# SiLU by one ScalarE function, and decay matrices of all heads formed beside the first stage and kept in DRAM

## The chip, the cores and the metric

The kernel runs on one core of a Trainium2 chip. The metric is the device time of one execution in microseconds, as the median of several runs. The engines are PE (TensorE, matrix products), DVE (VectorE), ACT (ScalarE), POOL (GpSimd) and SP (SyncE, which here only issues DMAs). Each works through its own instructions in the order of the program and waits on semaphores for the others. ACT and POOL issue DMAs too.

## The reference

One decoder block with two token mixers over 512 tokens of 2048 channels, in fp32: an mLSTM with 8 heads and a gated DeltaNet with 16 heads of 128 channels, which share one input projection and one output projection. Cut to what the change touches:

```python
def _causal_conv_silu(x, w):               # q, k and v of the DeltaNet
    y = sum(w[j] * xp[:, j:j + s] for j in range(kw))
    return jax.nn.silu(y)

# DeltaNet, per head: gam = cumsum of the log decay g over a chunk of 64 tokens
rel = gam[..., :, None] - gam[..., None, :]
decay_mat = jnp.where(incl, jnp.exp(jnp.where(incl, rel, 0.0)), 0.0)
a_mat = jnp.where(strict, bc[..., :, None] * kk * decay_mat, 0.0)
qk = jnp.einsum('cbhtd,cbhsd->cbhts', qc, kc) * decay_mat

# mLSTM, per head, with b the cumsum of log f and i the input gate
dmat = jnp.where(causal, bcum[..., :, None] - bcum[..., None, :] + ic[..., None, :], -jnp.inf)
intra_w = jnp.exp(dmat - m_t[..., None]) * scores
```

The decay matrices depend on the gates alone, which come from a narrow projection at the start; q, k and v are not needed for them. The kernel forms them in tiles of 128 tokens, so that a head has four matrices of 128x128, 256 KB together.

## The kernel before, in words

**Stages.** The front (0 to 135 us) loads x, forms the normalised `u`, the gates (`gates`) and a first part of q and k. The seven stage (135 to about 1105 us) computes the wide projections (output gates, SiLU paths, one part of q and k, v, merge gates). The mixers (to about 1870 us) run the heads in pairs beside the rest of the projections. The output stage (to about 2105 us) multiplies by the output weights.

**Products.** An fp32 weight tile is split in two parts of a shorter format: `wh` is ACT's cast (L143), `wl` DVE's difference (L146). Each product is then three matmuls, L614 with `wh` and the high part of `u`, L615 with `wl`, L616 with the low part of `u`.

**The seven stage** works through 13 blocks (`SEVEN`) of two column groups of 512; blocks 9 to 12 are the merge gates (kind "g"). A block replaces eight products of quarters by seven and has 16 quads of weights: eight A quads with four products each (m6, m1, m5, m7), then eight B quads with three. A product is six matmuls, two halves `t` of 128 rows by three, and takes 1.36 us; an A quad takes 5.44, a block 76.2. For an A quad DVE forms the sums `t` (128x1024, L555) and `ts` (128x512, L556) from the raw weights `wr`; ACT and DVE split `ts`, a part of `wr` and `t`. For a B quad DVE forms `ts` (L574), and the wide part is `wr` itself. The raw weights come through SP's queue into a ring of four buffers (tag "wr").

**Where a block turns.** The sums of products stand in banks `ps`: m6 in two, m1, m5 and m7 in two each, one for each half `t`. After the eighth A quad (the turn from A to B) ACT copies m6 to `X` (L599), and DVE adds m1, m5 and m7 to copies in `X` (L671), so that the B products can write the banks. At the end of a block the results are evacuated: those of m1 and m5 by ACT straight from the bank into a tile `to` (L682, `out_`), those of m7 by DVE into `X` and then ACT in place (L687, `late`). Each is stored with a DMA on ACT's queue, for the merge gates to `tg_d`. A tile `to` is a buffer of the same ring "wr" as the raw weights. The banks pass from block to block in turn: the m7 products of the next block write the banks that held m5.

**Order.** PE's instructions are written out by hand. The other engines' instructions are ordered by the scheduler from priorities (`urgent`, `behind`). `start(gen, ...)` runs a generator beside PE's products: `tick()` is called once for each product, and a `yield n` puts the rest off by n ticks. `beside[b]`, filled from `ahead`, is the generator that starts during block b; before, only the scaling of `u` and its loading back run in this way.

**Mixers.** `silu_end` takes a convolved tile to SiLU: with weights that were halved before, ACT's Tanh into `th` (L930), then DVE's (th + 1) · x (L931). `dn_front_k` broadcasts a head's row of `gam` to all partitions by a DMA on POOL's queue (`gb`), POOL masks it (L974, `affine_select`), ACT takes four exponentials of 128x128 (L985); the second head of a pair takes four of 64x64 more (L988), for a block of the matrix with its sign turned, and both one over the whole row (L990). `ml_head` does the same from `nrb` into `wm` (L1267, L1272).

## Time and profile before

| | us |
|---|---|
| median of 3 runs (lowest, highest) | 2138.02 (2137.24, 2138.37) |
| the profiled execution's own time | 2138.79 |
| its span, first to last instruction | 2137.0 |
| PE busy | 2117.4 (99%) |
| DVE busy | 1736.5 (81%) |
| ACT busy | 1084.7 (51%) |
| POOL busy | 473.1 (22%) |

The times in the trace start with the span, and an execution takes about 1.8 us more than it. Busy is the time in which an engine had an instruction under way; matmuls are pipelined, so a busy PE is not one at its peak. The granted clock of PE was 0.998 of full speed over the span. DMA moved 463 MB, 217 GB/s.

### The profile page before, as it was taken

The numbers are of one execution on the slowest core, as the hardware profiler recorded it, in microseconds if no ns is written. First come the engines' busy times: TensorE is split into PE (matmuls) and PEld (weight loads), VectorE is DVE, ScalarE is ACT, GpSimd is POOL, SyncE is SP. The second block draws the span as 40 slices with busy tenths as digits, with TensorE's granted clock in tenths as the row PEclk, the third lists the DMA queues.
The fourth block names the chain that finished last, engine by engine and source line by source line (L and its number), as shares of the span: only waits on it lengthen the run. The fifth ranks groups of instructions, "written<-read, shape, count | busy, mean of one in ns | idle before, by whom it ended". The sixth has DMA issues, their size and how long they took to land.

```text
span 2137.0 us, 32335 instructions
## 1 busy us (share of the span) xinstructions
PE 2117.4 (99%) x10555; PEld 1753.1 (82%) x10555; DVE 1736.5 (81%) x3024; ACT 1084.7 (51%) x2107; POOL 473.1 (22%) x681
## 2 busy tenths in 40 slices
PE   9999999999999999999999999999999999999998
PEld 7778888888888888888888888888888888887786
DVE  5988898898888888777857887887878888569887
ACT  4445555455554554444445556556465464345345
POOL 1210000000004000000003345345344363243211
PEclk9999999999999999999999999999999999999999
DMA  5456766677778877776987777678786678678895
GB/s 178 142 182 205 225 217 224 228 232 239 230 246 254 256 223 230 238 225 197 308 293 184 188 181 189 164 181 190 190 217 169 167 193 220 187 237 276 247 295 228
DMA packets 459203, 463.39 MB, mean 217 GB/s; under 512 B 198357, under 2 KB 306618, under 8 KB 458906
## 3 DMA queue, kind: packets, MB, share of 16 engines
q1 hardware_dynamic: 385466, 347.71, 56.4%
q0 software_dynamic: 25472, 75.26, 11.4%
q10 hardware_dynamic: 48096, 38.36, 5.4%
q8 instruction: 83, 1.36, 0.3%
q14 instruction: 86, 0.70, 0.1%
HBM read 359.41 MB, written 105.97 MB: 218 GB/s over the span
## 4 chain that ended last, share of the span: by engine, by line
PE 85%; DMA 3%; DVE 3%; issue 1%; ACT 1%; SPq 0%; POOL 0%; ACTq 0%; POOLq 0%; DVEq 0%
PE ps L615 17%; PE ps L614 17%; PE ps L616 17%; PE pj L265 14%; PE pj L263 7%; PE py L1494 2%; PE py L1496 2%; PE py L1495 2%; DMA ls<-ld 1%; DVE wl L146 1%; PE pqk L1077 1%; PE pnum L1300 1%; PE po L1189 1%; PE pw L1174 1%; PE pr L1166 1%
## 5 line engine op out<-in xcount | busy, mean ns | idle before, releaser
L143 ACT CAST wh<-wr 128x512 fp32r<-128x512 f32 (+1 forms) x522 | 374.2, 718 | 414.0 <-PE pj L265 199.3
L146 DVE TENSOR_TENSOR wl<-wr,wh 128x512 fp32r<-128x512 f32 (+1 forms) x522 | 442.3, 849 | 147.0 <-ACT wh L143 137.3
L263 PE MATMUL pj<-uh,wh 128*128 128x512 f32 x896 | 375.9, 420 | 1.3 <-ACT qk L379 1.3
L265 PE MATMUL pj<-uh,wl 128*128 128x512 f32 x896 | 351.4, 392 | 0.6 <-DVE wl L146 0.6
L265 PE MATMUL pj<-ul,wh 128*128 128x512 f32 x896 | 349.9, 390 | 0.3 <-DVE ul L330 0.3
L615 PE MATMUL ps<-wl,uh 128*128 128x512 f32 x752 | 292.7, 389 | 1.4 <-DVE wl L146 1.4
L614 PE MATMUL ps<-wh,uh 128*128 128x512 f32 x752 | 292.7, 389 | 0.8 <-DVE X L671 0.8
L616 PE MATMUL ps<-wh,ul 128*128 128x512 f32 x752 | 292.6, 389 | 0.0
L143 ACT CAST wh<-t 128x1024 fp32r<-128x1024 f32 x120 | 126.5, 1054 | 285.8 <-PE ps L616 153.3
L569 POOL DMA_DIRECT2D t_d<-ts x104 | 56.7, 545 | 863.8 <-DVE ts L556 831.7
L615 PE MATMUL ps<-wl,suh 128*128 128x512 f32 x624 | 242.9, 389 | 0.8 <-DVE wl L146 0.8
L614 PE MATMUL ps<-wh,suh 128*128 128x512 f32 x624 | 242.9, 389 | 0.2 <-ACT wh L143 0.2
L616 PE MATMUL ps<-wh,sul 128*128 128x512 f32 x624 | 242.7, 389 | 0.0
L143 ACT CAST wh<-ts 128x512 fp32r<-128x512 f32 x240 | 148.2, 618 | 173.9 <-DVE ts L574 149.0
L146 DVE TENSOR_TENSOR wl<-t,wh 128x1024 fp32r<-128x1024 f32 x120 | 146.9, 1224 | 77.2 <-ACT wh L143 77.1
L265 PEld LDWEIGHTS pj<-uh,wl 128*128 128x128 f32 x896 | 168.2, 188 | 37.0 <-DVE wl L146 1.0
L263 PEld LDWEIGHTS pj<-uh,wh 128*128 128x128 f32 x896 | 168.9, 188 | 31.1 <-ACT qk L379 1.8
L265 PEld LDWEIGHTS pj<-ul,wh 128*128 128x128 f32 x896 | 169.0, 189 | 30.6 <-DVE ul L330 1.1
L146 DVE TENSOR_TENSOR wl<-ts,wh 128x512 fp32r<-128x512 f32 x240 | 164.5, 686 | 21.0 <-ACT wh L143 19.5
L615 PEld LDWEIGHTS ps<-wl,uh 128*128 128x128 f32 x752 | 141.2, 188 | 31.2 <-DVE wl L146 2.0
L614 PEld LDWEIGHTS ps<-wh,uh 128*128 128x128 f32 x752 | 141.1, 188 | 30.6 <-DVE X L671 1.2
L616 PEld LDWEIGHTS ps<-wh,ul 128*128 128x128 f32 x752 | 141.1, 188 | 29.3
(363 smaller groups left out, 3898.0 us busy)
## 6 DMA issues: line engine op xcount, KB each, us to landing
wr<-in_w_in_dram SPq DMA_DIRECT2D x744, 256.0 KB, 3.9
wr<-in_w_out_dram SPq DMA_DIRECT2D x138, 256.0 KB, 4.7
t_d<-ts POOLq DMA_DIRECT2D x104, 256.0 KB, 3.8
wr<-t_d SPq DMA_DIRECT2D x104, 256.0 KB, 4.1
us_d<-uhi ACTq DMA_DIRECT2D x16, 256.0 KB, 3.5
us_d<-ulo ACTq DMA_DIRECT2D x16, 256.0 KB, 4.8
tg_d<-X ACTq DMA_DIRECT2D x16, 256.0 KB, 4.5
tg_d<-to ACTq DMA_DIRECT2D x16, 256.0 KB, 4.6
```

The costliest lines, as they stand in the source:

```text
L143: newest["A"] = A.copy(hi, src).ins
L146: newest["V"] = V.tensor_tensor(out=lo, in0=src, in1=hi.bitcast(F32), op=ALU.subtract).ins
L263: T.matmul(ps[j], hi[:, k, wsl], uh[:, kt, :], start=(kt == 0), stop=False)
L265: T.matmul(ps[j], w[:, k, wsl], x_[:, kt, :], start=False, stop=(kt == KT - 1 and w is lo))
L569: queue.dma_start(t2_d[b % 2, i], ts[:, 0, :])
L614: T.matmul(ps[t], ah, hi, start=(g == "A" and i == 0), stop=False, skip_group_check=True)
L615: T.matmul(ps[t], ah, lo, start=False, stop=False, skip_group_check=True)
L616: T.matmul(ps[t], al, hi, start=False, stop=(i == KH - 1), skip_group_check=True)
L1077: T.matmul(pk[:, c, :], kq[j][:, 0, tsl], kq[j][:, 1, tsl], start=True, stop=True)
L1494: T.matmul(ps[c], uh[:, kt, tsl], hi, start=(kt == ks[0]), stop=False)
L1495: T.matmul(ps[c], uh[:, kt, tsl], lo, start=False, stop=False)
L1496: T.matmul(ps[c], ul[:, kt, tsl], hi, start=False, stop=(kt == ks[-1]))
```

## The change

`silu_end` uses ACT's Silu in place, without DVE's multiplication and without the halved weights. The program has two table loads on ACT in place of one, the second ahead of the first Silu. A new generator `decay(n)` forms the decay matrices of head n in a buffer `spare(False)` of the ring "wr": the row's broadcast on POOL's queue, the mask on POOL three ticks later, the exponentials on ACT two ticks later, and a store to `dm_d` on ACT's queue. It runs for the 24 heads one after the other, six ticks each, from the eighth quad of block 9 on (`ahead[KH + 1]`). For the odd DeltaNet heads (`mirror`) it takes twelve exponentials, four of 64x128 and eight of 64x64, for the others four of 128x128. In the mixers `load_decay` loads them on SP's queue. `gates` takes the exponential of all `gam` rows once and stores it as rows 33 to 48.

```diff
     def silu_end(dst, then=None):
-        th = wkb.tile([P, S], F32, tag="th", name="th", bufs=2)
         with behind("A"):
-            A.activation(th, dst, AF.Tanh)
-        V.scalar_tensor_tensor(out=dst, in0=th, scalar=1.0, in1=dst, op0=ALU.add, op1=ALU.mult)
+            A.activation(dst, dst, AF.Silu)
...
         nc.scalar.dma_start(rows_d[16:32, :], gam)
+        A.activation(gr, gam, AF.Exp)
+        nc.scalar.dma_start(rows_d[33:49, :], gr)
...
+    def decay(n):
+
+        mirror = n < DNH and n % 2
+        bias, row = (ngam[:, :, n], 16 + n) if n < DNH else (acol[:, :, n - DNH], n - DNH)
+        flat = spare(False)
+        t = flat.rearrange("p (c t) -> p c t", t=P)
+        G.dma_start(flat, rows_d[row, :].partition_broadcast(P))
+        if mirror:
+            pgam = sbp.tile([P, NC], F32, tag="pgam", name="pgam", bufs=1)
+            G.tensor_scalar(out=pgam, in0=bias, scalar1=-1.0, scalar2=None, op0=ALU.mult)
+        yield 3
+        for a, b in (((0, 0), (64, 64)) if mirror else ((0, 0),)):
+            v = t[a:(a + 64 if mirror else P), :, b:P]
+            G.affine_select(out=v, in_=v, pattern=[[0, NC], [1, P - b]], channel_multiplier=-1, base=0,
+                            compare_op=ALU.is_ge, fill=-1e30)
+        yield 2
+        with behind("A"):
+            for c in range(NC):
+                if mirror:
+                    A.activation(t[0:64, c, :], t[0:64, c, :], AF.Exp, bias=bias[0:64, c:c + 1])
+                    A.activation(t[64:P, c, 64:P], t[64:P, c, 64:P], AF.Exp, bias=bias[64:P, c:c + 1])
+                    A.activation(t[64:P, c, 0:64], t[64:P, c, 0:64], AF.Exp, scale=-1.0, bias=pgam[64:P, c:c + 1])
+                else:
+                    A.activation(t[:, c, :], t[:, c, :], AF.Exp, bias=bias[:, c:c + 1])
+            nc.scalar.dma_start(dm_d[n], flat)
+        yield 1
+
     ahead = [None] + [scaled_u(k) for k in range(0, KT, 2)] + [None] * (len(SEVEN) - KH - 1)
+
+    def decays():
+        for n in range(DNH + MLH):
+            yield from decay(n)
+
+    ahead[KH + 1] = decays()
...
+    def load_decay(t, n):
+        with behind("S"):
+            nc.sync.dma_start(t.rearrange("p c t -> p (c t)"), dm_d[n])
...
     def dn_front_k(hs, kq, u):
-        rbs = [row_bcast(16 + h, "gb") for h in hs]
-        yield 4
+        rbs = [row_bcast(33 + h, "gb") for h in hs]
         for j in range(2):
             dm = wk.tile([P, NC, P], F32, tag="dm", name="dm")
-            G.affine_select(out=dm, in_=rbs[j], pattern=[[0, NC], [1, P]], channel_multiplier=-1, base=0,
-                            compare_op=ALU.is_ge, fill=-1e30)
+            load_decay(dm, hs[j])
             u["dm"].append(dm)
...
-            with behind("A"):
-                for c in range(NC):
-                    A.activation(dm[:, c, :], dm[:, c, :], AF.Exp, bias=ngam[:, c, h:h + 1])
-                if j:
-                    for c in range(NC):
-                        A.activation(dm[64:128, c, 0:64], rb[64:128, c, 0:64], AF.Exp, scale=-1.0,
-                                     bias=pgam[64:128, c:c + 1])
-                A.activation(rb, rb, AF.Exp)
...
-        rb = row_bcast(h, "nrb")
...
-        G.affine_select(out=w, in_=rb, pattern=[[0, NC], [1, P]], channel_multiplier=-1, base=0,
-                        compare_op=ALU.is_ge, fill=-1e30)
+        load_decay(w, DNH + h)
         yield 2
-        with behind("A"):
-            for c in range(NC):
-                A.activation(w[:, c, :], w[:, c, :], AF.Exp, bias=acol[:, c, h:h + 1])
```

Three places in ACT's order follow. In such rows a DMA waits for the last transfer that used its own semaphore, so that "DMAHW7" at a store says which semaphore it takes, and "DMAHW7" at a later row that it waits for this store. Lines of the changed kernel are numbered higher by three (L685 for L682, L690 for L687, L602 for L599). `to<-to` are the exponentials of `decay`, in a tile of the ring.

ACT at the end of block 9, before. The casts are those of the next block's first weights.

```order
L143 CAST wh<-t_7934 128x1024 [waits PE_49,Activation_49]
L687 ACTIVATE X<-X,bia 128x512 x2
L682 ACTIVATE to<-ps,bia 128x512 [waits PE_49] x2
...
L683 DMA tg_d<-to 128x512 [waits DMAHW5_49,Activation_49]
L682 ACTIVATE to<-ps,bia 128x512 [waits DVE_49]
...
L143 CAST wh<-t_8013 128x1024 [waits DVE_49,PE_49]
...
L682 ACTIVATE to<-ps,bia 128x512 [waits DVE_49]
L143 CAST wh<-ts 128x512 [waits DVE_49,PE_49]
L143 CAST wh<-wr_7923 128x512 [waits DMAHW2_49,PE_49]
...
L687 ACTIVATE X<-X,bia 128x512 [waits DVE_49] x2
```

The same place in the changed kernel; twelve exponentials (4 of 64x128, 8 of 64x64) stand just ahead of its first row.

```order
L144 CAST wh<-t_7990 128x1024 [waits PE_49,Activation_49]
L690 ACTIVATE X<-X,bia 128x512 x2
L685 ACTIVATE to<-ps,bia 128x512 [waits PE_49]
L685 ACTIVATE to<-ps,bia 128x512 [waits DMAHW6_49,PE_49]
L875 DMA dm_d<-to 128x512 [waits DMAHW7_49,Activation_49]
...
L686 DMA tg_d<-to 128x512 [waits DMAHW2_49,Activation_49]
...
L144 CAST wh<-t_8087 128x1024 [waits DVE_49,PE_49]
L685 ACTIVATE to<-ps,bia 128x512 [waits DMAHW7_49]
L874 ACTIVATE to<-to,ngam 128x128 [waits DMASW6_49,Pool_49]
...
L144 CAST wh<-ts 128x512 [waits DVE_49,PE_49]
L144 CAST wh<-wr_7979 128x512 [waits DMAHW6_49,PE_49]
L685 ACTIVATE to<-ps,bia 128x512 [waits DMAHW2_49]
```

The head's store stands behind the first evacuations, the evacuation of the first m5 bank waits for it (DMAHW7), and the next head's four exponentials stand between this evacuation and the last one.

ACT at the turn from A to B in block 10, before.

```order
L143 CAST wh<-ts 128x512 [waits DVE_49,PE_49,Activation_49]
L143 CAST wh<-wr_8258 128x1024 [waits DMAHW7_49,DMAHW0_49,PE_49]
L599 COPY X<-ps 128x512 [waits PE_49]
L599 COPY X<-ps 128x512 [waits DMAHW2_49,PE_49]
L143 CAST wh<-ts 128x512 [waits DVE_49,Activation_49]
L143 CAST wh<-wr_8303 128x1024 [waits DMAHW2_49,DMAHW3_49,PE_49,Activation_49]
```

And in the changed kernel, where nine more exponentials of the same three kinds are left out after the fourth row.

```order
L144 CAST wh<-wr_8393 128x1024 [waits DMAHW7_49,DMAHW0_49,PE_49]
L870 ACTIVATE to<-to,ngam 64x128 [waits DMASW6_49,Pool_49]
L871 ACTIVATE to<-to,ngam 64x64 [waits Pool_49]
L872 ACTIVATE to<-to,pgam 64x64 [waits Pool_49]
...
L871 ACTIVATE to<-to,ngam 64x64
L602 COPY X<-ps 128x512 [waits PE_49]
L872 ACTIVATE to<-to,pgam 64x64
L602 COPY X<-ps 128x512 [waits PE_49]
L144 CAST wh<-ts 128x512 [waits DVE_49]
```

The two copies, which stood directly behind the cast of `wr`, now have eleven exponentials ahead of them and one between them.

ACT at the end of block 10, before.

```order
L143 CAST wh<-t_8590 128x1024 [waits PE_49,Activation_49]
L687 ACTIVATE X<-X,bia 128x512 x2
L682 ACTIVATE to<-ps,bia 128x512 [waits PE_49] x2
...
L683 DMA tg_d<-to 128x512 [waits DMAHW5_49,Activation_49]
L682 ACTIVATE to<-ps,bia 128x512 [waits DVE_49]
...
L143 CAST wh<-t_8669 128x1024 [waits DVE_49,PE_49]
...
L682 ACTIVATE to<-ps,bia 128x512 [waits DVE_49]
L143 CAST wh<-ts 128x512 [waits DVE_49,PE_49]
```

And in the changed kernel; six more exponentials of the same kinds are left out ahead of the first evacuation.

```order
L690 ACTIVATE X<-X,bia 128x512 x2
L870 ACTIVATE to<-to,ngam 64x128 [waits DMASW6_49,Pool_49]
L871 ACTIVATE to<-to,ngam 64x64 [waits Pool_49]
L872 ACTIVATE to<-to,pgam 64x64 [waits Pool_49]
...
L685 ACTIVATE to<-ps,bia 128x512 [waits PE_49]
...
L685 ACTIVATE to<-ps,bia 128x512 [waits DMAHW3_49,PE_49]
...
L685 ACTIVATE to<-ps,bia 128x512 [waits DVE_49]
...
L686 DMA tg_d<-to 128x512 [waits DMAHW3_49,Activation_49]
L144 CAST wh<-ts 128x512 [waits DVE_49,PE_49]
...
L690 ACTIVATE X<-X,bia 128x512 [waits DVE_49]
...
L685 ACTIVATE to<-ps,bia 128x512 [waits DMAHW3_49]
```

Nine exponentials stand between the two `X` and the first evacuation, and the last evacuation waits for the store of the first one's tile (DMAHW3) and stands behind the casts and both `X`.

## Rows read from the trace of the kernel before

**Rows 1.** Busy time by stage: window, length, each engine, clock, DMA share, GB/s.

```profile
core 0: us, PE busy (x) PEld busy (x) DVE busy (x) ACT busy (x) POOL busy (x), PEclk, DMA share, GB/s
0.00:135.00 135.00, 128.91 (x603) 103.54 (x604) 105.18 (x188) 60.99 (x108) 24.99 (x34) 1.00 0.53 160
842.00:1105.00 263.00, 263.00 (x1162) 217.78 (x1161) 202.47 (x254) 122.90 (x171) 13.87 (x32) 1.00 0.76 248
1105.00:1870.00 765.00, 764.18 (x4557) 638.36 (x4556) 606.81 (x1489) 416.11 (x1109) 302.88 (x408) 1.00 0.74 189
1870.00:2105.00 235.00, 232.07 (x1022) 190.13 (x1021) 191.55 (x264) 107.82 (x170) 66.58 (x95) 1.00 0.87 273
```

**Rows 2.** What PE waited for: us in total, times, longest.

```profile
PE ps L614 <- DVE X L1518: 0.7, 2, 0.5
PE pr L1166 <- DVE st L1185: 0.7, 2, 0.4
```

**Rows 3.** Lines of ACT and DVE: busy us, mean ns of one, idle before.

```profile
L985 ACT ACTIVATE dm<-dm,ngam 128x128 f32<-128x128 f32 x64 | 20.3, 389 | 0.0
L988 ACT ACTIVATE dm<-gb,pgam 64x64 f32<-64x64 f32 x32 | 8.5, 332 | 0.2
L930 ACT ACTIVATE th<-kq 128x512 f32<-128x512 f32 x32 | 20.1, 627 | 4.0 <-DVE kq L924 3.9 <-issue 0.2
L277 ACT ACT_TABLE_LOAD x1 | 1.3, 1283 | 1.3 <-DVE warm L276 1.3
L931 DVE SCALAR_TENSOR_TENSOR kq<-th,kq 128x512 f32<-128x512 f32 x32 | 23.1, 720 | 0.9 <-ACT th L930 0.9
```

**Rows 4.** Timeline of ACT around 875: start, length, instruction, idle before.

```profile
871.09 0.62 ACT L143 CAST wh<-wr 128x512 fp32r<-128x512 f32 x1
...
873.45 1.05 ACT L143 CAST wh<-t 128x1024 fp32r<-128x1024 f32 x1 [1.74 <-PE ps L616]
874.40 1.33 ACT L687 ACTIVATE X<-X,bia 128x512 f32<-128x512 f32 x2
...
878.62 0.68 ACT L682 ACTIVATE to<-ps,bia 128x512 f32<-128x512 f32 x1
...
889.71 1.06 ACT L143 CAST wh<-t 128x1024 fp32r<-128x1024 f32 x1 [3.35 <-PE ps L616]
```

**Rows 5.** Timelines of DVE and PE, the rows that the walks need.

```profile
886.50 0.68 DVE L146 TENSOR_TENSOR wl<-ts,wh 128x512 fp32r<-128x512 f32 x1
...
883.39 0.39 PE L614 MATMUL ps<-wh,suh 128*128 128x512 f32 x1
889.51 0.39 PE L614 MATMUL ps<-wh,suh 128*128 128x512 f32 x1
...
925.55 0.39 PE L614 MATMUL ps<-wh,uh 128*128 128x512 f32 x1
...
959.55 0.39 PE L614 MATMUL ps<-wh,suh 128*128 128x512 f32 x1
```

**Rows 6.** DMA issues: out<-in, queue, count, size, median us to landing.

```profile
tg_d<-to ACTq DMA_DIRECT2D x16, 256.0 KB, 4.6
gz_d<-to ACTq DMA_DIRECT2D x8, 256.0 KB, 2.3
v_d<-to ACTq DMA_DIRECT2D x8, 256.0 KB, 7.3
...
wr<-in_w_in_dram SPq DMA_DIRECT2D x12, 256.0 KB, 3.4
...
wr<-in_w_in_dram SPq DMA_DIRECT2D x11, 256.0 KB, 4.8
```

**Rows 7.** Timelines of ACT and DVE at the turn in block 10.

```profile
917.87 1.06 ACT L599 COPY X<-ps 128x512 f32<-128x512 f32 x2
...
922.14 1.88 DVE L671 TENSOR_TENSOR X<-X,ps 128x512 f32<-128x512 f32 x3
923.93 1.22 DVE L146 TENSOR_TENSOR wl<-wr,wh 128x1024 fp32r<-128x1024 f32 x1
```

**Rows 8.** Timeline of ACT at the end of block 10.

```profile
950.56 1.34 ACT L687 ACTIVATE X<-X,bia 128x512 f32<-128x512 f32 x2
```

**Rows 9.** Busy time in two stretches of the last blocks.

```profile
1030.00:1040.00 10.00, 10.00 (x45) 8.27 (x45) 8.69 (x12) 6.00 (x9) 1.08 (x2) 1.00 1.01 341
1040.00:1060.00 20.00, 20.00 (x90) 16.55 (x89) 15.23 (x19) 7.88 (x12) 2.18 (x4) 1.00 0.99 346
```

More of the change, by code (lines that the diff above doesn't have):

```diff
@@ L84, in hybrid_body @@
     dr = ctx.enter_context(tc.tile_pool(name="dr", bufs=1, space=DRAM))
-    rows_d = dr.tile([33, S], F32, tag="rows", name="rows_d")
+    rows_d = dr.tile([49, S], F32, tag="rows", name="rows_d")
     h_d = dr.tile([KT, 16, BS, 4, BS], F32, tag="hd", name="h_d")
+    dm_d = dr.tile([DNH + MLH, P, S], F32, tag="dmd", name="dm_d")
     hm_d = dr.tile([KT, 16, BS, 4, BS], F32, tag="hmd", name="hm_d")
@@ L134, in turn_taps @@
         nc.sync.dma_start(rows_d[32, :].rearrange("(c t) -> c t", t=P), rr)
-        V.tensor_scalar(out=convc, in0=pt[:, 0:192], scalar1=0.5, scalar2=None, op0=ALU.mult)
+        V.tensor_copy(convc, pt[:, 0:192])
         V.tensor_scalar(out=normc[:, 16:32], in0=pt[:, 192:208], scalar1=0.125, scalar2=None, op0=ALU.mult)
@@ L969, in dn_front_k @@
     def dn_front_k(hs, kq, u):
[L970 to L971 removed]
+        rbs = [row_bcast(33 + h, "gb") for h in hs]
         for j in range(2):
             dm = wk.tile([P, NC, P], F32, tag="dm", name="dm")
[L974 to L975 removed]
+            load_decay(dm, hs[j])
             u["dm"].append(dm)
[L977 to L979 removed]
+        yield 7
         for j in range(2):
[L981 removed]
             ge = wk.tile([P, NC], F32, tag="ge", name="ge", bufs=4)
[L983 to L992 removed]
+            G.tensor_copy(ge, rbs[j][:, :, P - 1])
+            u["dm"][j] = (u["dm"][j], rbs[j], ge)
         nk = wk.tile([P, 2, NC], F32, tag="nk", name="nk")
```

6 lines of the change are left out of this document (removed).

## The prediction

> **What bounds the kernel now.** I read the busy shares by stage first. TensorE (PE) is busy for 263.00 of 263 us in the last part of the seven stage, for 764.18 of 765 in the mixers and for 232.07 of 235 in the output stage [rows 1]; at a PE clock of 1.00 there. So PE is the bound in every stage that the change touches, and what a relieved engine can give back is PE's idle time beside it: 0.82 us in the mixers, 2.93 in the output stage, 3.75 together. The view of what PE waited for agrees: in these stages it names waits of half a microsecond, on VectorE (DVE), and none on the selects or exponentials that the change removes [rows 2]. PE's instructions stand in the same order in both kernels. The question is therefore only which waits of PE go, and which come.
>
> **What the change removes.** In the mixers, 64 and 32 exponentials of the DeltaNet heads, 20.3 and 8.5 us of ScalarE (ACT), and 32 of the mLSTM heads; of each of the 48 SiLUs the multiplication on DVE, while ACT's own part stays one instruction [rows 3]. GpSimd (POOL) loses 24 selects. In the mixers DVE is busy for 606.81 of 765 us, ACT for 416.11 and POOL for 302.88 [rows 1]: none of them bounds. I credit half of the 0.82 us, −0.4, with bounds of −3.75 (all idle of both stages goes) and 0. In the place of the selects come 24 loads of 256 KB on SP's queue. They are written ahead of their use by seven ticks and more, their source was stored before the mixers begin, and they wait for tile buffers whose last reader belongs to an earlier unit: 0, up to +2 if a weight load behind them on SP comes late. ACT's second table load takes 1.28 us by the first [rows 3], beside 349 us in which ACT has nothing to do in the mixers (765 − 416.11): 0 while PE's next weights are already split, 1.3 if not.
>
> **What it adds in the first stages.** In the gates one exponential over 512 columns, 0.62 us by the SiLU's row of that length [rows 3], and one store. PE is idle for 6.1 of the first 135 us [rows 1], so the front is not as tight as the later stages; if this is on its path it is worth all of it: +0.3, between 0 and 0.6.
>
> The decays are 160 exponentials in 196 us beside blocks 9 to 12. Four of 128 columns in a row take 20.3/16 = 1.27 us, so one each 0.293 after the other; four of 64 columns 8.5/8 = 1.06, one each 0.243 [rows 3]. A plain head costs ACT 1.3 us, a mirrored one (4 of 128 and 8 of 64 columns) 3.2. In a steady A quad ACT is idle for 3.35 us before each cast of `t` [rows 4], and the split of `ts` (the DVE row at 886.50) ends 2.3 us before the product that takes it starts at 889.51 [rows 5]. So exponentials between the casts of `t` and `ts` cost nothing if they are below that, and those of plain heads are. ACT works in order, so what counts is where a mirrored head falls on a place without such slack. The printed order has three.
>
> **Block 9 to 10.** Twelve exponentials stand behind the cast of `wr`, which ends at 871.7 [rows 4]; 3.2 us later, at 874.9, comes the cast of `t`, which before began at 873.45. It and the two `X` (0.95 and 1.2) end at 877.0, the two evacuations at 878.3. The head's store is issued when the exponentials are done and the queue reaches it, about 875.9. Now the evacuation of the first m5 bank takes the buffer that this store frees, and waits for its landing: with 4.6 us, as stores of `to` to tg_d land [rows 6], at 880.5. It ends at 881.2. Behind it the order has four more exponentials (1.2), two `X` (1.2), the casts of `ts` and `wr` (1.05): the evacuation of the second m5 bank starts at 884.6 and ends at 885.3. Before, it was done at 879.3 [rows 4], and PE puts the second m7 product of the new block, which writes that bank, at 883.39 [rows 5]. Wait: 2.0 us (the first m5 bank, free at 881.2, is in time for the product 0.68 earlier). Bounds: if the store lands in 2.3 us, the cast of `t` ahead of the evacuation decides, since DVE still has to split the late one (1.22) and form the next (1.22), and everything is 0.4 earlier: 1.6. At 7.3 us it is 2.7 later: 4.6 [rows 6].
>
> **The turn from A to B in block 10.** The two copies `X<-ps` follow the cast of `wr` at 917.87 before. Eleven exponentials of a mirrored head now stand between (4 × 0.293 + 7 × 0.243 = 2.9 us) and one more between the copies: copies at 920.7 and 921.5. DVE's chain behind them is an add at 921.4; the second behind the second copy at 922.1, ending 922.8; a third, 0.6; the split of `ts`, 0.6; two adds, 1.2; then the split of the wide `wr` (1.14 to the next) and the next `ts` (0.6), which the new order puts ahead of the last add. That ends at 927.6, where before the sixth add ended at 924.0 [rows 7]. PE puts the product that writes this bank at 925.55 [rows 5]. Wait: 2.0; 3.2 if exponentials don't overlap (0.39 and 0.33 each [rows 3], +1.2), 1.4 if the last add gets done ahead of that `ts`.
>
> **Block 10 to 11.** Two `X` from 950.56 [rows 8], then nine exponentials (2.4 us), the evacuations, with one exponential between. The first ends at 954.9; its store goes out behind the others at about 955.6, and the last evacuation, in its buffer, waits for the landing: 960.2, done at 960.9. PE needs it at 959.55 [rows 5]: 1.4. With 2.3 us ACT's own queue decides (evacuation 959.9 to 960.6): 1.0; with 7.3, 4.1. At the third boundary and the next turn a plain head of 1.3 us stands in the way, and the second copy's margin of 1.5 us (924.0 to 925.55) covers it: 0.
>
> A wait that PE has served covers the following one: after it, every engine is that much ahead, so mirrored heads between `t` and `ts` just behind a boundary (3.2 against 2.3 + 2.0) add nothing.
>
> **Sum.** 2.0 + 2.0 + 1.4 + 0.3 − 0.4 = **+5.3 us** on the profiled execution's 2138.79. It lies 0.77 above the median, so I predict 2138.02 + 5.3 = **2143.3**. Low end: 1.6 + 1.4 + 1.0 + 0 − 3.75 = +0.25. High end: 4.6 + 3.2 + 4.1 + 0.6 + 2 = +14.5.
>
> **A rule weighed.** The row broadcasts and the stores of the decays are 48 transfers of 0.262 MB in 196 us, 64 GB/s, on top of 248 at a share of 0.76 [rows 1]: 0.96 of the DMA engines in proportion. The rows show what a full share does: loads of weights land in 3.4 us at 1000 to 1020, in 4.8 at 1040 to 1060, where the share is 0.99, and PE doesn't wait in either [rows 6, 9]. The Trainium skill, "DMA: Bandwidth & Descriptors", section "Issuing engines are not separate DMA queues", says that transfers started by ACT, SP or GpSimd all run on the same 16 engines and interleave. By that rule moving the stores to ACT's queue spares nobody: the weights would be late too. The rows agree that landing grows with the share.
>
> **Rivals.**
> 1. *No difference* (within 0.2%, 4.3 us, which is about what a measurement here tells from none). The three waits are real but at their low bounds, 4.0 us, and the mixers give 0.4 back: +3.6, 2141.6. For it: stores of `to` to gz_d landed in 2.3 us [rows 6], and two of my three margins are known to half a microsecond. Against it: the turn needs no store at all.
> 2. *Contention.* Each landing in the walks grows by 1.4 us, as from 3.4 to 4.8: the two boundaries wait 1.4 longer each, +8.1, 2146.1; and from 1030 on, where the share was full before, the last heads come on top. Against: PE had no wait at a share of 0.99. The Trainium skill's rule named above is what would make it come out so.
> 3. *Late in the mixers.* A load of a decay waits on SP for its buffer, and the loads of weights behind it land late; it decides once SP is held for longer than the splits are ahead. At 0.3 to 0.5 us for a third of the 16 DeltaNet loads, +2 and more: 2145.3 up. For it: mixer loads go through SP alone. Against: the order has each behind loads whose buffers are as old.
> 4. *Faster* (the other side). The exponentials' place in the mixers was what made PE's last half microseconds there, and in the first stage they fit: the waits above don't come, because ACT, whose idle time ahead of the cast of `t` at 873.45 was 1.74 us [rows 4], catches up before the banks are needed. Then 3.75 us is all that PE has to give: 2134.3 at best, below 0.2%; it needs idle time in the front besides (135 − 128.91 = 6.1) to be told from no change, and the gates get longer there.
>
> **Chances.** The forecast (+4.3 to +6.5) 0.42, contention 0.11, late mixers 0.04: slower 0.57. No difference 0.38, the slower half of it at 2141 to 2142.3. Faster 0.05. The forecast's own range is 2142 to 2145; the range that holds 8 in 10 runs from 2138 (the low end) to 2150, short of the high end, since not all bounds fall together.
>
> **What would show it.** In the profile after: PE idle for 5 to 6 us in 842 to 1105, as three waits that begin near 883, 928 and 964 (each later by what went before), the first and third named after ACT's evacuation or its store (a DMA to dm_d or tg_d), the second after DVE's `X`; ACT's evacuations behind dm_d's landing; no new wait above 0.5 us in the mixers. Wrong, if PE stays at no idle there, if the waits name loads of `wr`, or if the mixers' idle rises above 2 us.

## The result and the profile after

The changed kernel takes 2151.96 us, the median of four runs (2150.91 to 2152.59), where four runs of the kernel before, on the same chip, had 2138.11: a ratio of 1.0065, with an interval from 1.0048 to 1.0082. It is slower by 13.9 us. The forecast was slower by 5.3, so the sign was right and the size was not: the time lies above the forecast's range (2142 to 2145) and above the wider one (to 2150). The profiled execution took 2152.59, its span is 2150.8 and its granted clock 0.997. Of all the runs below, one, of the kernel "spread, and scaling later", took 2645.60 us at a granted clock of 0.752 and is left out of that kernel's median.

Two statements ahead of the prediction were wrong. At the turn in block 10 seven exponentials are left out in the listed order, not nine. And the raw weights of the seven stage have a ring of their own ("wr3", three buffers); the ring "wr" of four buffers serves in blocks 9 to 12 only the tiles `to` of the evacuations and, with the change, the decays. A decay thus takes buffers from evacuations and not from weights.

Below, "the first stage" is the part of the seven stage from 842 us on, blocks 9 to 12. PE's order is the same in both kernels, so the start of the same matmul in both traces tells where time is lost. In the changed kernel it starts 0.49 us earlier where 842 us stood before, 4.26 later at 900, 8.07 later at 940, and 11.86 later at 1105; from there to 1870 this grows to 14.73, and at the end it is 14.2. So the front gives 0.5, the first stage loses 12.4, the mixers 2.9, and the output stage gives 0.5.

The view of busy time by stretch shows the same. The columns are those of [rows 1]: stretch, length, busy time of PE, PEld, DVE, ACT and POOL, granted clock, DMA share, GB/s.

```profile
842.00:1117.00 275.00, 267.54 (x1161) 219.13 (x1160) 209.20 (x254) 172.13 (x330) 51.15 (x85) 0.99 0.83 279
1117.00:1885.00 768.00, 764.27 (x4558) 638.20 (x4557) 573.95 (x1441) 374.96 (x966) 272.48 (x368) 1.00 0.75 194
...
886.10:889.00 2.90, 2.87 (x7) 2.29 (x8) 1.60 (x4) 2.06 (x3) 0.74 (x2) 0.50 0.90 149
...
971.00:975.00 4.00, 4.00 (x13) 3.11 (x12) 3.33 (x5) 2.98 (x7) 2.00 (x2) 0.57 0.86 251
```

Against [rows 1] PE is idle for 7.5 us in the first stage (275 − 267.54), where it was idle for none, and for 3.7 in the mixers, where it was 0.8. The last two rows are two stretches behind waits: the granted clock is 0.50 and 0.57 of full speed, 0.50 being the lower of the two levels, 1.2 of 2.4 GHz.

The view of what PE waited for names the places: us in total, times, longest.

```profile
PE ps L617 <- ACT to L685: 4.8, 2, 3.0
PE ps L617 <- DVE X L674: 3.2, 3, 1.7
...
PE pw L1199 <- DVE r L1194: 1.7, 1, 1.7
...
PE p L1169 <- DVE s L1163: 1.1, 1, 1.1
PE pr L1191 <- DVE st L1210: 0.9, 1, 0.9
```

The first line is two of the three foreseen waits; the second is the third of them, another beside it at the same turn, and one of 0.8 us in the output stage. The last three lines are in the mixers and were not foreseen; of these [rows 2] has only the one for `st`, at 0.7. PE's timeline shows the waits of the first stage (start, length, instruction, idle before).

```profile
886.13 0.79 PE L617 MATMUL ps<-wh,suh 128*128 128x512 f32 x1 [3.04 <-ACT to L685]
886.72 0.63 PE L618 MATMUL ps<-wl,suh 128*128 128x512 f32 x1
887.15 0.63 PE L619 MATMUL ps<-wh,sul 128*128 128x512 f32 x1
...
927.32 0.50 PE L617 MATMUL ps<-wh,uh 128*128 128x512 f32 x1 [0.74 <-DVE X L674]
...
933.47 0.50 PE L617 MATMUL ps<-wh,uh 128*128 128x512 f32 x1 [1.72 <-DVE X L674]
...
969.59 0.50 PE L617 MATMUL ps<-wh,suh 128*128 128x512 f32 x1 [1.80 <-ACT to L685]
```

Behind the first wait seven matmuls start 0.43 us apart (886.72, 887.15), not 0.23: that is the half clock, worth about 1.4 us there and, over nine matmuls, 1.8 at the end of block 10. Behind the waits at the turn the clock stays full (1.00 from 926 to 940).

ACT's timeline shows why the banks come late: at the end of block 9, at the turn (from 922.13) and at the end of block 10 (from 959.82). The row at 876.27 is the store of the head.

```profile
872.14 0.40 ACT L870 ACTIVATE to<-to,ngam 64x128 f32<-64x128 f32 x1
872.55 0.35 ACT L871 ACTIVATE to<-to,ngam 64x64 f32<-64x64 f32 x1
872.81 0.33 ACT L872 ACTIVATE to<-to,pgam 64x64 f32<-64x64 f32 x1
873.15 0.41 ACT L870 ACTIVATE to<-to,ngam 64x128 f32<-64x128 f32 x1
...
876.20 1.05 ACT L144 CAST wh<-t 128x1024 fp32r<-128x1024 f32 x1
876.27 0.33 ACTq L875 DMA_DIRECT2D dm_d<-to  x1
...
881.37 0.69 ACT L685 ACTIVATE to<-ps,bia 128x512 f32<-128x512 f32 x1 [0.15 <-DMA dm_d<-to]
...
885.40 0.68 ACT L685 ACTIVATE to<-ps,bia 128x512 f32<-128x512 f32 x1
...
890.30 1.06 ACT L872 ACTIVATE to<-to,pgam 64x64 f32<-64x64 f32 x4 [1.44 <-DMA to<-rows_d]
891.91 1.29 ACT L870 ACTIVATE to<-to,ngam 64x128 f32<-64x128 f32 x4 [0.54 <-POOL to L864]
893.21 1.06 ACT L871 ACTIVATE to<-to,ngam 64x64 f32<-64x64 f32 x4
...
922.13 0.40 ACT L870 ACTIVATE to<-to,ngam 64x128 f32<-64x128 f32 x1
...
925.96 0.59 ACT L602 COPY X<-ps 128x512 f32<-128x512 f32 x1
...
926.94 0.59 ACT L602 COPY X<-ps 128x512 f32<-128x512 f32 x1
...
959.82 0.39 ACT L870 ACTIVATE to<-to,ngam 64x128 f32<-64x128 f32 x1
...
962.87 0.69 ACT L685 ACTIVATE to<-ps,bia 128x512 f32<-128x512 f32 x1
```

Twelve exponentials take from 872.14 to 876.20, 4.06 us. A group of three is 1.01: from the wide one to the next 0.41, then 0.26, then 0.34. Only the two of 64x64 overlap. The next such head, at 890.30, has its twelve in three groups of equal ones, and they take 1.06 + 1.29 + 1.06 = 3.41 us: the order of the shapes makes 0.65. The evacuation behind the store waits 0.15 us for it, so that the store's landing hardly mattered; the time of ACT, and of DVE for the cast of `t` ahead, did.

By the rows of ACT's lines (busy us, mean ns of one) the changed kernel's exponentials and its Silu cost by themselves what those of before did: of [rows 3] the 128x128 has 389 ns, the 64x64 has 332, the Tanh 627.

```profile
L870 ACT ACTIVATE to<-to,ngam 64x128 f32<-64x128 f32 x32 | 12.6, 402 | 0.8 <-POOL to L864 0.5
...
L872 ACT ACTIVATE to<-to,pgam 64x64 f32<-64x64 f32 x32 | 10.4, 333 | 1.5 <-DMA to<-rows_d 1.4
...
L874 ACT ACTIVATE to<-to,ngam 128x128 f32<-128x128 f32 x32 | 10.3, 392 | 0.7 <-POOL to L864 0.7
...
L969 ACT ACTIVATE kq<-kq 128x512 f32<-128x512 f32 x32 | 20.1, 627 | 3.9 <-DVE kq L964 3.9
```

### The profile page after: what moved, and what is told of

Read it like the earlier page. It is cut to its first block, busy times and chain, and to the rows that moved or that the text cites. A ratio compares the mean times of both kernels' runs of the same rounds, so it can differ in the third digit from the quotient of the medians.

```text
span 2150.8 us, 32436 instructions
## 1 busy us (share of the span) xinstructions
PE 2122.4 (99%) x10555; PEld 1755.0 (82%) x10555; DVE 1712.1 (80%) x2976; ACT 1095.4 (51%) x2125; POOL 487.4 (23%) x705
## 5 line engine op out<-in xcount | busy, mean ns | idle before, releaser
L147 DVE TENSOR_TENSOR wl<-wr,wh 128x512 fp32r<-128x512 f32 (+1 forms) x522 | 437.4, 839 | 165.1 <-ACT wh L144 156.6
L144 ACT CAST wh<-t 128x1024 fp32r<-128x1024 f32 x120 | 126.6, 1055 | 256.2 <-PE ps L619 135.2
```

Of the source, the lines that this page charges most:

```text
L144: newest["A"] = A.copy(hi, src).ins
L147: newest["V"] = V.tensor_tensor(out=lo, in0=src, in1=hi.bitcast(F32), op=ALU.subtract).ins
```

## The experiments

Two questions stood: what makes the first stage lose 12 us, and why the mixers, which were relieved of work, lose 3. For the first, theory A was ACT's order: exponentials stand ahead of casts and evacuations on an engine that works in order, in its narrow form at three places alone. Its rival was the traffic: the 48 transfers of the decays delay weights, whatever ACT does. For the mixers the candidates were the loads of the decays on SP's queue, the SiLU, and a moved order of DVE's instructions.

The table gives for each kernel the median and its ratio to the kernel before, run on the same chip, and from the profiled execution how much later PE stands than before: gained over the first stage (842 to 1105) and over the mixers (1105 to 1870). These two columns are of one execution each; two of the same program, in the first two rows, differ by 1.1 us in the first stage and by 0.1 in the mixers.

| kernel | median us | ratio (interval) | first stage | mixers |
|---|---|---|---|---|
| the change | 2151.96 | 1.0065 (1.0048 to 1.0082) | 12.4 | 2.9 |
| the change, once more | 2151.85 | one run | 11.3 | 3.0 |
| SiLU alone | 2148.12 | 1.0044 (1.0031 to 1.0056) | 0.0 | 7.3 |
| decays alone | 2162.57 | 1.0110 (1.0094 to 1.0126) | 11.0 | 14.0 |
| one exponential a head | 2144.83 | 1.0033 (1.0021 to 1.0044) | 3.4 | 3.1 |
| heads apart from the turns | 2152.22 | 1.0059 (1.0046 to 1.0071) | 10.5 | 3.8 |
| four exponentials for every head | 2147.53 | 1.0046 (1.0032 to 1.0060) | 5.3 | 3.7 |
| exponentials spread | 2141.86 | 1.0021 (1.0012 to 1.0031) | 1.2 | 2.8 |
| loads on POOL's queue | 2151.86 | 1.0068 (1.0054 to 1.0081) | 9.2 | 2.9 |
| spread, and scaling later | 2144.83 | 1.0028 (1.0017 to 1.0039) | 0.7 | 2.4 |
| decays alone, scaling later | 2152.63 | 1.0071 (1.0055 to 1.0086) | 10.3 | 3.5 |
| before, with table loads | 2146.44 | 1.0042 (1.0028 to 1.0056) | 0.0 | 9.2 |
| spread, scaling later, POOL's queue | 2140.04 | 1.0012 (1.0002 to 1.0021) | 1.4 | 1.3 |

**SiLU alone**, without the decays and without the halved weights:

```diff
-        th = wkb.tile([P, S], F32, tag="th", name="th", bufs=2)
...
-            A.activation(th, dst, AF.Tanh)
-        V.scalar_tensor_tensor(out=dst, in0=th, scalar=1.0, in1=dst, op0=ALU.add, op1=ALU.mult)
+            A.activation(dst, dst, AF.Silu)
```

> The kernel before with the SiLU part alone. Theory A (the waits of the changed kernel come from the decays: in the first stage from exponentials that stand ahead of evacuations of banks, and in the mixers, 2.9 us, from the loads of decays on SP's queue): no new wait anywhere, 2136.5 to 2138.5 us. Rival C (the 2.9 us of the mixers come from SiLU: its table load, or tiles that come at another time): 2140 to 2141.5 us, with new waits of PE after 1105 us and none before.

It is slower by 10 us, all of it behind the first stage. Rival C had the place, but no theory had the size. ACT's lines name what had been overlooked (busy us, mean ns of one):

```profile
L929 ACT ACT_TABLE_LOAD x16 | 20.5, 1283 | 0.3
...
L983 ACT ACT_TABLE_LOAD x8 | 10.3, 1283 | 0.1
...
L1270 ACT ACT_TABLE_LOAD x7 | 9.0, 1283 | 0.1
```

With the exponentials still in the mixers, Silu and Exp take turns, and each turn loads a table: 31 loads and the first, 41 us of ACT, where the whole change has two loads. The Trainium skill, "ScalarE: Activation LUTs", section "What ACT_TABLE_LOAD costs", puts a load at about 1283 ns, and the rows agree. The 1380 ns of drain that it adds for every switch do not show here: in this trace each of the 31 loads starts 0.02 us behind the instruction ahead of it, and in 30 cases the next starts 0.01 us behind the load (0.46 in the other), so that a switch takes ACT 1.3 us and not 2.7.

**Decays alone**, the change with the Tanh, DVE's product and the halved weights kept.

```diff
...
-            A.activation(dst, dst, AF.Silu)
+            A.activation(th, dst, AF.Tanh)
+        V.scalar_tensor_tensor(out=dst, in0=th, scalar=1.0, in1=dst, op0=ALU.add, op1=ALU.mult)
```

> The changed kernel with the old SiLU (Tanh, DVE's multiplication, halved weights), so the decays alone. Theory A: the whole loss stays, 2150.5 to 2153 us, 12 us of it in 842 to 1105 and 2 to 4 in the mixers. Rival C: only the 12 us of the first stage, 2148.5 to 2150 us.

The first stage loses 11.0, as expected: it is the decays' own. The mixers lose 14, which was not. The view of PE's waits names it:

```profile
PE p L1171 <- DVE s L1165: 7.8, 5, 1.7
```

The two parts alone cost 10 and 24 us and together 14. They need each other: the decays take the exponentials out of the mixers, so that Silu switches no tables; and with DVE's instructions in the order that the scheduler chose, the mixers with the decays lose 14.0 us with the multiplication on DVE and 2.9 without it.

**One exponential a head**, so that ACT's time for the decays goes from 1.3 or 4.1 us to 0.62 and every transfer stays. Bias and sign of the decay matrices are left out.

```diff
-            for c in range(NC):
-                if mirror:
...
+            A.activation(flat, flat, AF.Exp)
```

> The changed kernel with one exponential over 512 columns (0.62 us, without bias) in the place of the 4 or 12 of each head; all transfers, masks and stores stay. It leaves the decay matrices wrong by the bias. Theory A (ACT's time ahead of the evacuations): PE's new waits in 842 to 1105 fall from 12.3 us to under 2, 2139 to 2142.5 us. Rival B (48 more transfers make weights and buffers late): at least 8 us stay, 2148 us and more.

The first stage loses 3.4, not 12.4. So ACT's exponentials make about 9 of the 12 us (half clock included), and transfers, masks and stores together at most the rest. Theory A had at most 2 us left, its rival at least 8; what stays is nearer to A.

**Heads apart from the turns.** The heads keep their instructions and start at ticks that avoid the turns and the block ends.

```diff
+        t0, slots = clock["t"] - 4 * (KH - 1), (0, 6, 12, 18, 32, 38, 44)
+        at = [56 * b + s for b in range(4) for s in slots][4:]
         for n in range(DNH + MLH):
+            if t0 + at[n] > clock["t"]:
+                yield t0 + at[n] - clock["t"]
             yield from decay(n)
```

> The changed kernel with each head's start put off to one of seven ticks of a block, so that no exponentials stand around the turn from A to B or the end of a block; the same exponentials, transfers and buffers. Theory A: the three waits go, at most 1 us in 842 to 1105, and the mixers keep their 2.9: 2139 to 2142 us. Rival B: the same bytes, so at least 8 us stay: 2148 us and more.

The narrow form of A fell. The three waits are gone, and the first stage still loses 10.5, as the rival had it, in other places. PE's waits from 842 to 1115 us, 5.4 in all; behind both places, near 897 and 1055, the clock falls as well (0.63 from 898.9 to 902.0), which makes most of the rest:

```profile
PE ps L618 <- DVE wl L147: 2.8, 4, 1.4
PE ps L617 <- ACT wh L144: 2.6, 2, 1.9
```

ACT's timeline shows the first of them:

```profile
886.25 0.62 ACT L144 CAST wh<-wr 128x512 fp32r<-128x512 f32 x1
891.28 1.05 ACT L872 ACTIVATE to<-to,pgam 64x64 f32<-64x64 f32 x4 [4.41 <-issue]
...
894.73 1.05 ACT L144 CAST wh<-t 128x1024 fp32r<-128x1024 f32 x1
...
884.48 0.55 POOL L857 DMA_DIRECT2D to<-rows_d  x1 [4.50 <-DMA tg_d<-to]
```

ACT stands for 4.41 us at an exponential whose row has not arrived (the trace has its landing at 891.20), and the cast of `t` behind it, at 894.73, is the one PE waits for. The last row is POOL's: the broadcast of that row could be issued at 884.48 only, when the store of an evacuation had freed its buffer. So the general form stays: whatever stands ahead of a cast on ACT, be it exponentials or the wait of one, delays the cast.

**Four exponentials for every head**, none mirrored (the sign-turned block is left out).

```diff
-        mirror = n < DNH and n % 2
+        mirror = False
```

> The changed kernel with four exponentials of 128x128 for the eight mirrored heads too, in place of twelve (it leaves out the block with the sign turned). Mirrored heads then take ACT 1.3 us in place of 4.1. Theory A (the first-stage waits are ACT's time in the wrong places): the waits at the end of block 9, the turn in block 10 and the end of block 10 fall to 1 us or less each, no stretch at half clock behind them, 842 to 1105 loses 3 to 5 us in place of 12.3; 2141.5 to 2144.5 us. Rival B (transfers and buffers): 10 us and more stay there, 2150 us.

The first stage loses 5.3. So the mirrored heads' longer group makes about 7 of the 12 us, but plain heads are not free, as the prediction had them: PE waits 1.6 us for an evacuation, 1.3 for `wl` and 1.2 for `wh`, and the clock stays full.

**Exponentials spread.** The same instructions, with the row fetched nine ticks ahead of the first exponential, a quarter of the head's exponentials in each of four ticks, and two heads in flight, away from the turns.

```diff
...
-        yield 3
+        yield 6
...
-        yield 2
-        with behind("A"):
-            for c in range(NC):
+        yield 3
+        for c in range(NC):
+            with behind("A"):
...
+            yield 1
...
+        t0, slots = clock["t"] - 4 * (KH - 1), (4, 8, 12, 16, 29, 34, 39)
...
-            yield from decay(n)
+            if t0 + at[n] > clock["t"]:
+                yield t0 + at[n] - clock["t"]
+            start(decay(n))
```

> The changed kernel with each head's exponentials spread over four ticks (one chunk of 128 each), its broadcast nine ticks ahead of them, two heads in flight, and no head in the ticks around the turn and the end of a block. ACT then never has more than about 1.6 us of exponentials between two casts, and none waits for its broadcast. Theory A, with what e6 showed added (ACT also stood behind an exponential whose row had not landed): 842 to 1105 loses at most 1.5 us, the mixers 2 to 3: 2140 to 2143 us. Rival B (48 transfers more): as with e6, 8 us and more stay in 842 to 1105, 2148 us and more.

The first stage loses 1.2 us. The stretch, and PE's only named wait in it:

```profile
842.00:1108.00 266.00, 265.65 (x1171) 218.99 (x1170) 209.57 (x253) 173.25 (x332) 52.82 (x87) 1.00 0.88 287
```

```profile
PE ps L617 <- DVE X L674: 0.3, 1, 0.3
```

ACT is as busy as in the change (173.25 against 172.13 us) and the DMA share is higher (0.88 against 0.83). Neither ACT's load nor the traffic as such is the cost, then; the cost is what stands ahead of a cast or an evacuation for which PE has no time left. It is not the length of a run alone: two runs of nine exponentials remain here (863.62 to 866.65 is one), and in the change runs of twelve at 853.47 and 942.26 hold up nothing. Three things changed together, shorter runs, other places and rows fetched early; other places alone (10.5 above) and short runs alone (5.3 with four exponentials) were not enough, and what each is worth here is not shown. The median falls by 10 us; the mixers stay at 2.8.

**Loads on POOL's queue**, for the mixers: the loads of the decays no longer stand on SP's queue.

```diff
-            nc.sync.dma_start(t.rearrange("p c t -> p (c t)"), dm_d[n])
+            nc.gpsimd.dma_start(t.rearrange("p c t -> p (c t)"), dm_d[n])
```

> The changed kernel with the decays loaded by the mixers on POOL's queue in place of SP's. Theory D (the wait of 1.9 us near 1349 comes from a load of 256 KB ahead of the stores td<-to on SP's queue): that wait goes, first stage as with the change, 2149 to 2151 us. Rival E (the mixers' 2 to 3 us come from another order of DVE's work, vt scaled ahead of aq): the wait near 1349 may stay or go, but those near 1766 and 1781 stay, 2151 to 2153 us.

The mixers lose 2.9 as before, by other waits: the one for `s` near 1766 is gone, the one for `r` near 1349 is 1.0 (1.7 in the change), the one for `st` is 1.5 (0.9 in the change). So neither theory D nor rival E has it whole, and SP's queue alone is not the cause.

**Scaling later.** PE waits for `s` in the mixers, and `s` follows on DVE a chain that begins with `aq`. DVE's order has changed around it. In DVE's order before (rows between are left out), `aq` (`pk` times the decay) stands ahead of the scaling of `vt`, in the changed kernel behind it:

```
before:   L1004 aq<-pk,dm     L146 wl<-wr,wh     L1116 vt<-vt,nk x2
changed:  L147 wl<-wr,wh      L1141 vt<-vt,nk x2     L1029 aq<-pk,dm
```

The timeline of DVE shows it, in the first two rows before, in the others in the changed kernel:

```profile
1392.34 0.69 DVE L1004 TENSOR_TENSOR aq<-pk,dm 128x512 f32<-128x512 f32 x1 [0.24 <-PE pk L1002]
...
1737.20 0.69 DVE L1004 TENSOR_TENSOR aq<-pk,dm 128x512 f32<-128x512 f32 x1 [0.91 <-PE pk L1002]
...
1406.42 1.48 DVE L1141 TENSOR_TENSOR vt<-vt,nk 128x512 f32<-128x512 f32 x2
1407.83 0.68 DVE L1029 TENSOR_TENSOR aq<-pk,dm 128x512 f32<-128x512 f32 x1
...
1752.39 0.68 DVE L1029 TENSOR_TENSOR aq<-pk,dm 128x512 f32<-128x512 f32 x1
```

Before, the `aq` of 1407.83 stood at 1392.34. It is 15.5 us later, where PE's matmuls are 13.8 later: the chain begins 1.7 us late, of which the scaling is 1.4. Here the chain still has room, and `s` comes in time. In the unit of the one wait for `s`, at 1766, `aq` comes at 1752.39 for 1737.20, 15.2 us later where PE is 12.4 later: 2.8 late, too much. `vt` is needed only later, so the scaling was put one step down, first into the decays alone, where the wait was longest, and into the spread kernel:

```diff
-        for j in range(2):
-            vn = u["vs"][j]
-            with behind("V"):
-                V.tensor_tensor(out=vn, in0=vn, in1=bc(u["nk"][:, j, :], P), op=ALU.mult)
         yield 2
         p2 = psw.tile([P, 2, 2 * NC, BS], F32, tag="wk", name="p2")
...
         yield 3
+        for j in range(2):
+            vn = u["vs"][j]
+            with behind("V"):
+                V.tensor_tensor(out=vn, in0=vn, in1=bc(u["nk"][:, j, :], P), op=ALU.mult)
```

> The kernel of e2 (decays alone, old SiLU) with the same edit of DVE's order. e2 lost 14 us in the mixers, most of it in five waits of 1.4 to 1.9 us of p for s. Theory E: these five waits fall to 0.5 us or less each, the mixers lose 4 to 7 us: 2151 to 2156 us. Rival (the loads of decays, or DVE's load as such): at least 11 us stay there, 2159 us and more.

In the decays alone the mixers' loss falls from 14.0 to 3.5 us and the median by 10. PE's waits for `s`, to be read against the 7.8 above:

```profile
PE p L1171 <- DVE s L1165: 1.8, 5, 0.5
```

> The kernel of e7 with one more edit: in the mixers the scaling of vt is written one step later, so that DVE has both products aq<-pk,dm and their diagonals ahead of it; before the change the first stood ahead of it, with the change none. Theory E (the mixers' loss is this order: DVE's chain aq, diagonal, cs, which ends in s for PE's product p, starts 1.8 us later): the wait of p near 1757 goes, the mixers lose 0 to 1.5 us in place of 2.8; 2138.5 to 2141 us. Rival (the mixers' loss is the loads of decays or late stores): 2141 to 2143 us, as e7.

In the spread kernel the wait for `s` falls from 1.1 to 0.3, but the mixers still lose 2.4, with 1.3 at `st`, where theory E had at most 1.5. Its median, 2144.83, is above that of the spread kernel, but the intervals of the two ratios overlap, and the lowest runs of both are at 2140.6. Its profile has a wait of 1.9 us for a `wl` near 2050, in the output stage, with a lower clock behind it (0.65 from 2051.5 to 2056). Waits of 1.1 to 1.7 us for a `wl` in the output stage appear in the kernel before too (1.4 at 2002) and in five others, in the change 0.8 at most (1.0 in its repeat): what sets them off is open.

**Before, with table loads.** The kernel before with one Silu of a single column ahead of each Tanh, so that tables switch as in SiLU alone, and nothing else changes.

```diff
+        tiny = wkb.tile([P, 1], F32, tag="tiny", name="tiny", bufs=1)
         with behind("A"):
+            A.activation(tiny, dst[:, 0:1], AF.Silu)
             A.activation(th, dst, AF.Tanh)
```

> The kernel before with one Silu of a single column into a scratch tile ahead of each Tanh of the mixers, its result unused. ACT then changes its table as often as in e1 (SiLU alone: 32 table loads), while SiLU is computed as before. Theory T (SiLU alone costs what its table loads cost, since the exponentials of the mixers take turns with it): 5 to 10 us in the mixers, 2143 to 2148 us. Rival (e1's loss comes from Silu in place or from DVE's other order): 2138 to 2140 us.

The mixers lose 9.2, and PE's waits are of the kinds of SiLU alone, for `s` (3.4 against 2.5) and for ACT's `v` (2.2 against 0.9). The switches of tables, with the 48 small Silus of 0.2 us that cause them here, are enough to explain what SiLU alone loses, in size. One wait of SiLU alone, 1.8 us for `st` near 1773, does not come here, so not all of its loss goes the same way.

**The change once more**, unedited, to see which waits come again.

> The changed kernel once more, unedited, for what repeats in it. In its first profile PE ran at half clock for seven matmuls behind the wait of 3.2 us at the end of block 9 and for nine behind the wait of 2.0 at the end of block 10, 3 us together; in kernels with the same first stage (e2, e8, e11) the same waits were followed by such a stretch in one case of six. If the stretch belongs to the wait, it comes again and 842 to 1105 loses 12 us; if it is chance, it comes after one wait or none and the loss is 9 to 11 us.

The waits do: 3.0, 0.7, 1.7 and 1.8 us, as in the rows of the change. The half clock does in part. Its stretches behind the first and third wait:

```profile
886.10:890.00 3.90, 3.81 (x17) 3.16 (x18) 3.25 (x5) 2.20 (x5) 1.49 (x4) 1.00 0.84 179
970.00:975.00 5.00, 5.00 (x17) 4.01 (x16) 4.43 (x5) 1.92 (x5) 2.14 (x2) 0.67 0.92 322
```

This time the clock is full behind the first and low behind the third.

**Spread, scaling later, POOL's queue**: all three edits.

> The kernel of e9 (exponentials spread, DVE's order of before) with the mixers' loads on POOL's queue. If what is left in the mixers (2.4 us in e9, the largest a wait of 1.1 us near 1340 for stores that SP issues behind a load) is SP's queue, 1 us or less is left there, 2139 to 2141 us. If it is another thing (the order of the rest of DVE's work, or landings), 2 us and more stay: 2141 to 2143 us.

At 2140.04 it is the fastest version with the change, 12 us below it, and 0.1% above the kernel before (1.0002 to 1.0021). Its mixers:

```profile
1106.00:1872.00 766.00, 764.00 (x4556) 637.75 (x4555) 579.31 (x1442) 374.86 (x967) 290.18 (x391) 1.00 0.76 195
```

PE is idle for 2.0 us there, against 0.8 in [rows 1]. The loss in the mixers, 1.3 us, lies between the two answers that were set for it. No version with the change is faster than the kernel before.

## Why the prediction was right in sign and wrong in size

**Right.** PE was the bound, and what the change takes from DVE, POOL and ACT in the mixers gave PE nothing. The loss was foreseen where it came, as waits at the end of block 9, at the turn in block 10 and at its end, the first and third named after ACT's evacuations, the second after `X`. For the mixers its own signs went against it: it wanted no new wait above 0.5 us there, and there were three (1.7, 1.1 and 0.9), and it called itself wrong if the idle time there rose above 2 us, and it was 3.7. For the first stage the clue was to walk ACT's order past the banks that PE needs next; the shares of busy time show no hint of it (ACT 122.90 of 263 us, [rows 1]).

**The first stage: 5.4 foreseen, 12.4 measured.** The steps that failed are the price of a mirrored head and a clock and a late weight that were put at nothing. What was mis-sized, item by item:
- *The price of a mirrored head*, "four of 64 columns 8.5/8 = 1.06, one each 0.243 […] a mirrored one […] 3.2". It took 4.06. The rows behind the 3.2, [rows 3], were of four alike in a row, which overlap by 0.1 us each; in the new order the shapes alternate, and of three only two overlap. The head at 890.30, grouped by shape, takes 3.4. The same step is in all three walks: 12 exponentials 4.06 for 3.2 (rows at 872.14 and 876.20), 11 at the turn 3.8 for 2.9, 9 at the end of block 10 3.0 for 2.4. That is 0.9 + 0.9 + 0.6 = 2.4 us. The own upper bound for the turn, "3.2 if exponentials don't overlap", was nearer.
- *The clock.* No term was foreseen for a clock that falls behind a wait: 1.4 + 1.8 = 3.2 us.
- *A late weight* ahead of block 9's end, about 0.4. The walk let the exponentials start at 871.7; they started at 872.14, and PE's matmuls stood 0.5 us earlier than before, so against PE the start was 0.9 late, and about half of that was still there at the end of the chain. DVE's `t` had waited for its weight to land, which it did not before:

```profile
868.63 1.23 DVE L558 TENSOR_TENSOR t<-wr 128x1024 f32<-128x1024 f32 x1 [0.72 <-DMA wr<-in_w_in_dram]
```

  This wait, of 0.72 to 0.96 us, is in all five profiles with this first stage.
- *The front*, credited with +0.3, is not settled: at 842 us PE stands from 1.0 us earlier to 1.6 later than before in kernels with the same front, and block 9's wait is 3.0 us wherever it stands.
- *The rest at the turn*, about 0.8: the second copy came 0.98 us behind the first, not 0.8, and a `ts` on DVE took 1.05 to the next instruction, not 0.6. The walk had one late bank at the turn; the first bank of the B products was late too (the 0.74 in the row at 927.32), but that wait only took a part of the same lateness earlier.

The store's landing, on which the walk at block 9 and its bounds (2.3 to 7.3 us) rested, decided 0.15 us: it came 5.1 us after the issue at 876.27, and ACT's cast of `t`, behind DVE's sum and split, ended 0.15 us before it. The prediction had 0.4 between the two chains. At the end of block 10 ACT's own queue decided: no wait for a store stands ahead of the last evacuation.

Plain heads at "0" held in the change, where no wait falls on one, but not by themselves: with four exponentials for every head the stage loses 5.3. "A wait that PE has served covers the following one" is probably what kept them free; no run tests it by itself.

**The mixers: −0.4 foreseen, +2.9 measured.** The step that failed is the credit itself, that relief of engines which do not bound can only give. The scheduler placed DVE's instructions anew, and the scaling of `vt` moved ahead of `aq`. The prediction had looked at the order of ACT and PE, not of DVE there. That this order can cost the mixers 10 us is shown for the decays alone. With the change whole, in the spread kernel, the same edit took 0.8 us from the wait for `s` and 0.4 from the mixers in all; with the loads on POOL's queue as well it took 1.5. So for the change's own 2.9 us the cause is shown only in part. What is left, 1.3 to 2.4 us, falls on waits for `r` and `st` (0.8 and 1.1 with all three edits). In the change the one for `r`, near 1349, comes after DVE has stood 5.6 us for the landing of stores to `td`; why these land late is open.

**The rivals.** *Contention* did show in landings: from 870 to 900 weights land in 6.4 us at the median, before in 3.8. So the rows agree with the rule of the Trainium skill that the prediction named: with more transfers on ACT's and POOL's queues, SP's take longer. PE paid little for it: in the change the late weight above, with one exponential a head at most 3.4 us, and in the spread kernel the share is 0.88, weights land in 5.5 us in that stretch, and PE waits 0.3. *Late in the mixers* had about the right size, by its own mechanism at most in part: off SP's queue the loss stays the same until DVE's order is mended too. *No difference* and *faster* did not come.

## What to carry to other kernels

When work is moved beside a stage whose engine is half idle, look not at its idle share but at what stands ahead of each cast or evacuation, how long it takes or waits there, and how soon PE needs what comes behind: the same exponentials cost 12 us in runs of up to twelve wherever they fell, and 1 us in runs of mostly one to six (two of nine), away from the turns and with their inputs fetched early. Neither the place alone nor short runs alone did it. Price a run from rows of the same sequence of shapes, not from rows of equal ones. And an edit under a scheduler moves engines that it does not touch: compare the order on every engine, above all where an instruction without haste can slip ahead of the head of a chain.

## What was not expected of the hardware

- Exponentials of four alike overlap by 0.1 us each (four of 128x128 in 1.28 us, 0.392 each by itself); where the tile of 64x128 on the first 64 rows is followed or preceded by one of 64x64 on the last 64, they do not (0.41 and 0.34 us from start to start at 0.402 and 0.333 by themselves). The change of shape alone does not do it. In the changed kernel's mixers ACT multiplies tiles of 64x64 and 128x64 in turn, both from the first row on, and they start 0.24 us apart:

```profile
1416.08 0.34 ACT L1047 ACTIVATE aq<-aq,cs 64x64 f32<-64x64 f32 x1
1416.32 0.34 ACT L1048 ACTIVATE aq<-aq,cs 128x64 f32<-128x64 f32 x1
```

  So the change of the first row is what is left to suspect; no run here tests it by itself.
- Behind a wait of 1.8 or 3.0 us at a block's end the granted clock fell to the lower level for seven to nine matmuls in four of ten such places, in five profiles of kernels with the same first stage: both in the change, one in its repeat, one with the decays alone, none in the two others. Waits of 1.3 to 1.7 us at the turn never had it. The same program thus differs by 1 to 2 us from one execution to the next, and a single profile's cost of a wait is good to that only. In the kernel with the loads on POOL's queue, which has none of it, the first stage loses 9.2, in the change 12.4.
- A table switch that is off the critical path by busy shares (ACT is busy for about 60% of the mixers in SiLU alone) still cost 0.2 to 0.3 us of the mixers' time each (7.3 and 9.2 us for 31): PE's waits there name ACT's `v` and the chain to `s`.
